# Down projection of a gated FFN: Strassen sums of the weights and of the gated width made by adding transfers, with turned signs

## The chip, the cores and the metric

The kernel runs on one core of one Trainium2 chip. The metric is device time in microseconds (us) of one execution, start to end; lower is better. Engines are named as the profile names them: PE (matrix unit; PEld is its weight loading), DVE (vector), ACT (scalar), POOL (GpSimd) and SP (the queue that issues most transfers). "SPq" is SP issuing a transfer.

## The reference, cut to what matters

One transformer layer on 1024 tokens of width 1024. Only its last part is touched by the change:

```python
def conv_ffn(h, w_up, conv_w, conv_b, w_down):          # h (1, 1024, 1024)
    u = h @ w_up                                        # (1, 1024, 5632)
    acc = conv_b + sum(up[:, j:j + L] * conv_w[j] for j in range(3))   # width-3 depthwise conv over tokens
    a, g = jnp.split(acc, 2, axis=-1)                   # two halves of 2816
    return (jax.nn.silu(g) * a) @ w_down                # the gated width (1, 1024, 2816) @ (2816, 1024)
...
x = x_mid + g2 * conv_ffn(modulate(rms_norm(x_mid, norm2_w), sh2, sc2), w_up, conv_w, conv_b, w_down)
```

All of it is float32. The kernel splits every operand into a high and a low part, so each product of two blocks is three matmuls.

## The kernel before, in words

The stages follow each other: start-up, attention, mLSTM, the two branch projections, the output projection (`project`), and then, in `stage_ffn`, the up projection in 22 **units** and the down projection in 7 **products**.

A unit j (loop `for j in range(NFC)`, NFC = 22) makes 128 channels of `a` and 128 of `g`. `Units.first_mm`, `first_ev` and `rest` run the seven block products of a Strassen scheme on PE into the banks `pa`, `pc`, `pb`; ACT and DVE bring them to the tiles `ua` and `ug` (128 channels x 1024 tokens). `conv_gate(j, ua, ug)` puts the convolution on DVE and ACT (tiles `cv`), multiplies, and stores the gated 128 x 1024 block to the HBM tensor `f_d`. The weights of a unit come in one 1 MB load to a tile `ur`. While the conv of unit j runs on DVE, PE is already in unit j + 1.

The tiles `ua`, `ug`, `cv` and those of the sums come from one pool of eight buffers (`ur`/`accp`, tag "a"), six of them allocated a unit. So what is stored or summed late holds back a tile of about the unit after next.

The down projection multiplies the gated width F (2816 x 1024, in NK = 11 pairs of 128-row blocks k and NK + k, and two token halves `t0`, `t1`) by W (`w_dn`, two column halves). Seven products p = 0..6 read f_d, s1_d, s2_d (HBM: sums of F) and `w_dn` or T (HBM, `wt_d`: four sums of W for each k) in pieces of two k, which `operands` loads and splits. The sums are made during the units:

- `weight_sums(k, ...)`: loads four 128 x 512 blocks of `w_dn`, four DVE subtractions (helper line L1906, 128 x 512 each), four stores to T (L1945). For k = 0, 1, 2 (`E.w_early`) this runs in the output projection, with the loads on ACT's queue; for k = 3..10 in unit k + 1 with all on SP.
- `hidden_sums(k, fb)`, in units 12 to 21 and after the last: loads block k of f_d back (`fa`), four DVE operations on 128 x 512 (L2182 to L2185), two 512 KB stores to s1_d and s2_d.

A framework's scheduler sets the order of each engine's instructions when the program is built, and each engine then takes its instructions in that order. A transfer that has to wait stands at the head of its queue and holds back those behind it.

Of the kernel before, what the change touches and what calls it, by code (L numbers as in the profile page):

```python
# [8 lines left out]
F32 = mybir.dt.float32  # L9
# [4 lines left out]
ALU = mybir.AluOpType  # L14
# [4 lines left out]
P = 128  # L19
D = 1024  # L20
L = 1024
# [14 lines left out]
NFC = DFF // P  # L36
# [1566 lines left out]
def stage_tail(E, st):  # L1603
    nc, tc, A, ident, expo, vecT, dr, out, dbg = E.nc, E.tc, E.A, E.ident, E.expo, E.vecT, E.dr, E.out, E.dbg
# [45 lines left out]
    def x512(name, dt=F32R, pool=None):  # L1650
        if pool is None:
            pool = nx[0] % 56 // 8
            nx[0] += 1
        return xts[pool].tile([P, 512], dt, tag="x", name=name)
# [211 lines left out]
    def square(b, n=1):  # L1866
        if n == 0:
            RS[b] = tp1.tile([P, 4], F32, name=f"rrx{b}")
        rr = RS[b]
        sq = nc.scalar.activation(xj, acc[b][:, n * 512 : (n + 1) * 512], AF.Square, accum_out=rr[:, n : n + 1])  # L1870
        if n == 0:
            return sq
        nc.vector.tensor_scalar(rr[:, 2:3], rr[:, 0:1], rr[:, 1:2], D * EPS, op0=ALU.add, op1=ALU.add)
        nc.gpsimd.tensor_tensor(rr[:, 3:4], rr[:, 2:3], expo[:, 0:1], op=ALU.pow)
# [57 lines left out]

    NK = NFC // 2
    T = dr.tile([P, 4, NK, 512], F32, name="wt_d")
    E.w_early = 3

    def weight_sums(k, a0, a1, b0, b1, eng=None):
        for w, i, o in ((a0, 0, k), (a1, 1, k), (b0, 0, NK + k), (b1, 1, NK + k)):
            (eng or nc.sync).dma_start(w, A["w_dn"][i, :, o])
        sub(a0, a1, a0)  # L1940
        sub(a1, b1, a1)
        sub(b1, b1, a0)
        sub(b0, b0, b1)
        for i, o in enumerate((a0, b1, a1, b0)):
            nc.sync.dma_start(T[:, i, k], o)  # L1945

    psc = E.psx_s
    U = Units(
# [7 lines left out]
    for i, b in enumerate((4, 5, 6, 7, 0, 1, 2, 3)):  # L1956
        project(0, b, w)
        if i == 3:
            held = E.og
        sq = square(b, 0)  # L1960
        if 2 <= i < 2 + E.w_early:
            with tc.issue_after(sq.ins):
                weight_sums(i - 2, *[x512(f"w{x}{i - 2}", F32, 5 + i % 2) for x in range(4)], eng=nc.scalar)
    norm_factors()
    with tc.issue_after(held.ins):
        w = load_w(A["w_o"][1], "wo1", g1b[:, 512:1024], raws=raw)
# [177 lines left out]
def stage_ffn(E, st):  # L2144
# [9 lines left out]

    def conv_gate(j, ua, ug):
        res = []
        for u, ch in ((ua, j), (ug, NFC + j)):
            r = ur.tile([P, L], F32, tag="a", name=f"cv{j}_{ch}")  # L2160

            def cw(i):
                return vecT[:, V_CW + 44 * i + ch : V_CW + 44 * i + ch + 1]

            nc.scalar.activation(r, u, AF.Identity, bias=vecT[:, V_CB + ch : V_CB + ch + 1], scale=cw(1))  # L2165
            nc.vector.scalar_tensor_tensor(r[:, 1:], u[:, : L - 1], cw(0), r[:, 1:], op0=ALU.mult, op1=ALU.add)
            nc.vector.scalar_tensor_tensor(r[:, : L - 1], u[:, 1:], cw(2), r[:, : L - 1], op0=ALU.mult, op1=ALU.add)
            res.append(r)
        a, g = res
        nc.scalar.activation(g, g, AF.Silu)  # L2170
        nc.vector.tensor_tensor(a, a, g, op=ALU.mult)
        nc.sync.dma_start(f_d[j * P : (j + 1) * P], a)
        return a


    t0, t1 = slice(0, 512), slice(512, 1024)
    tt = nc.vector.tensor_tensor

    def hidden_sums(k, fb):
        fa, o = [ur.tile([P, L], F32, tag="a", name=f"f{x}{k}") for x in "as"]  # L2180
        nc.sync.dma_start(fa, f_d[k * P : (k + 1) * P])
        tt(o[:, t0], fa[:, t0], fa[:, t1], op=ALU.subtract)  # L2182
        tt(fa[:, t1], fa[:, t1], fb[:, t1], op=ALU.add)
        tt(fa[:, t0], fa[:, t1], fa[:, t0], op=ALU.subtract)
        tt(o[:, t1], fb[:, t0], fa[:, t0], op=ALU.subtract)  # L2185
        nc.sync.dma_start(s1_d[k * P : (k + 1) * P], fa)
        nc.sync.dma_start(s2_d[k * P : (k + 1) * P], o)

    def rows(src, k0, cs):
        return lambda k, n: src[(k0 + k) * P : (k0 + k + n) * P, cs].rearrange("(k p) t -> p k t", p=P)  # L2190
# [20 lines left out]
    def operands(i):  # L2211

        p, k0, n = pieces[i]
        if i % 7 < 2:
            raw = rawp.tile([P, 2, D], F32, tag="raw", name=f"dr{i}")
            raw = raw[:, 0], raw[:, 1]
        else:
            raw = op4(f"drf{i}", F32), op4(f"drw{i}", F32)
        raw = [r.rearrange("p (k c) -> p k c", k=2) for r in raw]
        out = []  # L2220
        for r, src in zip(raw, PRODS[p]):
            nc.sync.dma_start(r[:, :n], src(k0, n))
        for k in range(n):
            pairs = []
            for r, x in zip(raw, "fw"):
                pr = [E.x512(f"d{x}{y}{i}_{k}", pool=homes[i % len(homes)]) for y in "hl"]
                split_from(nc, *pr, r[:, k])
                pairs.append(pr)
            out.append(pairs)
        return out  # L2230

    def sums(j, a):
        if 0 <= j < NK:
            if j >= E.w_early:
                weight_sums(j, *[w[:, t] for w in [ur.tile([P, L], F32, tag="a", name=f"w{x}{j}") for x in "ab"] for t in (t0, t1)])
        elif j >= NK:
            hidden_sums(j - NK, a)

    a = None
    for j in range(NFC):  # L2240
# [21 lines left out]
    U2 = [E.x512(f"u2_{c}", F32, 3) for c in range(4)]  # L2262
    U4 = [E.x512(f"u4_{c}", F32, 3) for c in range(4)]

    def finish(q, ps, add):

        r, ns = q
        ns = (t0, t1)[ns]
        xm = []
        for c in range(4):  # L2270
            x = dx.tile([P, 512], F32, tag="xm", name=f"xm{q}{c}")
            nc.sync.dma_start(x, xm_d[(4 * r + c) * P : (4 * r + c + 1) * P, ns])
            xm.append(x)
        for c in range(4):
            o = op2(f"o{q}{c}", F32)
            src = ps[c]
            if add is not None:
                tt(o, src, add[c], op=ALU.add)
                src = o
            tt(o, src, g2b[:, ns], op=ALU.mult)  # L2280
            tt(o, o, xm[c], op=ALU.add)
            nc.sync.dma_start(out[(4 * r + c) * P : (4 * r + c + 1) * P, ns], o)
# [32 lines left out]
    for p in range(7):  # L2315

        ps = banks[p] = banks[p - 2] if p in (2, 5, 6) else (yb if p % 2 else xb)(p)
        first = p not in (2, 5, 6)
        ops = []
        if p == 6:  # L2320
            XM = ahead((1, 0), U2)
        while ix < len(pieces) and pieces[ix][0] == p:
            ops += ready[ix] if ix < len(ready) else operands(ix)
            ix += 1
            for _ in range(2 if ix in (5, 8, 11) else 1 if 4 <= ix < 17 else 0):
                last_row()
            if ix == 17:
                for i in (6, 7):
                    mod_row(E, None, i, banks[1][3], U4[2])
                nc.sync.dma_start(g2b, E.g_d[1].to_broadcast([P, D]))  # L2330
            n0 = len(ops) - pieces[ix - 1][2]
            for k in range(n0, min(len(ops), NK - TAIL if p == 6 else NK)):
                (fh, fl), w = ops[k]
                for c in range(4):
                    cs = sl(c * P, P)
                    product(nc, ps[c], [(fh[:, cs], fl[:, cs])], [w], first and k == 0, k == NK - 1)
        if p == 0:
            for c in range(4):
                copy_act(nc, U2[c], ps[c])
        elif p == 1:  # L2340
            for c in range(4):
                tt(U2[c], ps[c], U2[c], op=ALU.add)
        elif p == 2:
            finish((0, 0), ps, None)
        elif p == 3:
            for c in range(4):
                tt(U4[c], ps[c], U2[c], op=ALU.add)
        elif p == 4:
            finish((1, 1), ps, U4)
        elif p == 5:  # L2350
            finish((0, 1), ps, U2)
        else:
            s0, s1 = sl(0, 256), sl(256, 256)
            o, tmp = op2("ol3", F32), op2("olt", F32)
            tt(tmp[:, s1], ps[3][:, s1], g2b[:, s1], op=ALU.mult)
            tt(XM[3][:, s1], XM[3][:, s1], tmp[:, s1], op=ALU.add)
            for c, s, bank in [(c, t0, ps[c]) for c in range(3)] + [(3, s0, ps[3]), (3, s1, banks[5][0])]:
                cs = sl(c * P, P)
                rhs = [(w[0][:, s], w[1][:, s]) for _, w in ops[-TAIL:]]
                product(nc, bank[:, s], [(f[0][:, cs], f[1][:, cs]) for f, _ in ops[-TAIL:]], rhs, s is s1)  # L2360
                r = o if c == 3 else op2(f"ol{c}", F32)
                tt(r[:, s], bank[:, s], g2b[:, s], op=ALU.mult)
                tt(r[:, s], r[:, s], XM[c][:, s], op=ALU.add)
                nc.sync.dma_start(out[(4 + c) * P : (5 + c) * P, s], r[:, s])
    sX.close()

# [82 lines left out]
```

## Time and profile before

| | |
|---|---|
| median of 3 runs | 1844.02 us (1841.78 to 1851.08) |
| the profiled execution | 1849.14 us, its span 1847.4 us |
| granted PE clock, mean over the span | 0.988 |
| PE busy | 1790.8 us, 97% of the span |
| DVE busy | 1425.9 us, 77% |
| ACT busy | 1069.8 us, 58% |
| POOL busy | 508.3 us, 28%; nothing after 1250 us |
| transfers | 342.47 MB, all issued by SP (314.47 MB) and ACT (26.22 MB), none by POOL |

The output projection lies at about 1125 to 1210 us, the units at 1229 to 1650 us, the down projection at 1650 to 1847 us. Times in rows of the trace are us from the span's start unless they are marked ns. In a row of a timeline stand start, length, engine, line and what is written from what; a time behind `[` is idle time of that engine before the row and what ended it.

### The profile page before, as it was taken

How to read it: one execution, taken by the hardware profiler on the slowest of the kernel's cores; microseconds unless marked ns; L12 is line 12 of the kernel's file. 1: busy time of each engine (PE TensorE's matmuls, PEld its weight loads, DVE VectorE, ACT ScalarE, POOL GpSimd, SP SyncE). 2: the span in 40 equal slices, each digit the busy share in tenths (PEclk: the TensorE clock that was granted, in tenths of full speed). 3: DMA queues.
4: the chain of work that ended last, by engine and by line, in shares of the span. 5: the costliest groups of instructions: out<-in, count | busy, mean ns of one | idle time of the engine just before them, and what ended most of it. 6: DMA issues, size and time to landing. Idle time of an engine off the chain costs nothing.

```text
span 1847.4 us, 27864 instructions
## 1 busy us (share of the span) xinstructions
PE 1790.8 (97%) x9207; PEld 1283.5 (69%) x9207; DVE 1425.9 (77%) x2864; ACT 1069.8 (58%) x2229; POOL 508.3 (28%) x747
## 2 busy tenths in 40 slices
PE   7989999999998899999999999999999999999999
PEld 3855555555554566656668887878888888888887
DVE  3858888888788686858687787698889898897665
ACT  4747877878787565645356462476444444465441
POOL 2467769587862530303010020000000000000000
PEclk9999999999999899999999999999999999999999
DMA  9747988888796625261359927322454544599751
GB/s 342 233 138 146 201 170 179 192 180 199 147 182 131 219 79 192 79 213 37 132 188 368 344 92 246 141 77 106 172 207 180 194 160 166 195 318 371 260 172 69
DMA packets 302193, 342.47 MB, mean 185 GB/s; under 512 B 176208, under 2 KB 200672, under 8 KB 299232
## 3 DMA queue, kind: packets, MB, share of 16 engines
q1 hardware_dynamic: 287648, 314.47, 56.3%
q10 hardware_dynamic: 14400, 26.22, 4.2%
q8 instruction: 72, 1.18, 0.3%
q14 instruction: 73, 0.60, 0.1%
HBM read 224.61 MB, written 76.16 MB: 163 GB/s over the span
## 4 chain that ended last, share of the span: by engine, by line
PE 78%; DVE 7%; DMA 4%; issue 3%; ACT 3%; POOL 3%; SPq 0%; ACTq 0%; DVEq 0%; POOLq 0%
PE g L706 8%; PE pq L706 6%; PE pa L2027 4%; PE pa L2029 4%; PE pa L2028 4%; PE po L706 3%; PE dx L2029 2%; PE dx L2027 2%; PE dx L2028 2%; PE pb L2027 2%; PE pb L2029 2%; PE pb L2028 2%; PE yb L2029 2%; PE yb L2027 2%; PE yb L2028 2%
## 5 line engine op out<-in xcount | busy, mean ns | idle before, releaser
L850 DVE CUSTOM_DVE_ANT_0 s<-s,maskA,nsink 128x640 f32<-128x640 f32 (+1 forms) x128 | 117.4, 917 | 65.5 <-PE s L845 65.0
L866 DVE TENSOR_TENSOR P<-s,P 128x640 f16<-128x640 f32 (+1 forms) x128 | 100.6, 786 | 1.0 <-ACT s L861 1.0
L860 ACT ACTIVATE P<-s,st 128x640 f16<-128x640 f32 (+1 forms) x128 | 98.2, 767 | 4.1
L706 PE MATMUL g<-hH,fh 128*128 128x512 f16 x256 | 97.1, 379 | 0.0
L706 PE MATMUL g<-hH,fl 128*128 128x512 f16 x256 | 97.0, 379 | 0.0
L706 PE MATMUL g<-hL,fh 128*128 128x512 f16 x256 | 97.0, 379 | 0.0
L861 ACT ACTIVATE s<-s,st 128x640 f32<-128x640 f32 (+1 forms) x128 | 93.8, 733 | 0.0
L706 PEld LDWEIGHTS <-hH 128*128 128x128 f16 x640 | 62.8, 99 | 37.3 <-issue 1.8
L858 ACT ACTIVATE st<-st,shift 128x1 f32<-128x1 f32 x128 | 37.6, 294 | 85.6 <-DVE st L850 84.8
L706 PE MATMUL pq<-wha,hH 128*128 128x384 f16 (+1 forms) x256 | 84.9, 332 | 0.1
L706 PE MATMUL pq<-wha,hL 128*128 128x384 f16 (+1 forms) x256 | 84.9, 332 | 0.0
L706 PE MATMUL pq<-wla,hH 128*128 128x384 f16 (+1 forms) x256 | 84.9, 332 | 0.0
L706 PEld LDWEIGHTS <-fh 128*128 128x128 f16 x512 | 49.2, 100 | 45.4
L2165 ACT ACTIVATE cv<-ua,vecT 128x1024 f32<-128x1024 f32 x22 | 27.4, 1246 | 84.9 <-DVE ua L2138 84.9
L1436 POOL TENSOR_SCALAR kwh<-k,gcall 128x128 fp32r<-128x128 f32 x72 | 32.5, 455 | 157.2 <-PE dC L164 53.9
L47 ACT ACTIVATE dfh<-drf 128x512 fp32r<-128x512 f32 x55 | 34.4, 628 | 59.3 <-PE dx L2028 26.5
L2027 PE MATMUL dx<-dwh,dfh 128*128 128x512 f32 (+1 forms) x176 | 68.3, 388 | 0.0
L2029 PE MATMUL dx<-dwh,dfl 128*128 128x512 f32 (+1 forms) x176 | 68.2, 388 | 0.0
L2028 PE MATMUL dx<-dwl,dfh 128*128 128x512 f32 (+1 forms) x176 | 68.2, 387 | 0.0
L54 DVE TENSOR_TENSOR dfl<-drf,dfh 128x512 fp32r<-128x512 f32 x55 | 37.6, 688 | 36.1 <-ACT dfh L47 36.1
L165 PE MATMUL kv<-whkv,hL 128*128 128x384 f16 x192 | 62.6, 326 | 0.0
L164 PE MATMUL kv<-wlkv,hH 128*128 128x384 f16 x192 | 62.6, 326 | 0.0
(691 smaller groups left out, 6249.9 us busy)
## 6 DMA issues: line engine op xcount, KB each, us to landing
ur<-in_w_up SPq DMA_DIRECT2D x22, 1024.0 KB
wmb<-in_w_modB SPq DMA_DIRECT2D x48, 256.0 KB
f_d<-cv SPq DMA_DIRECT2D x22, 512.0 KB
wm<-in_w_modA SPq DMA_DIRECT2D x16, 512.0 KB
fr<-in_w_g SPq DMA_DIRECT2D x32, 256.0 KB
drf<-fs_d SPq DMA_DIRECT2D x15, 512.0 KB
drw<-wt_d SPq DMA_DIRECT2D x14, 512.0 KB
w1b<-in_w_cx SPq DMA_DIRECT2D x16, 388.0 KB
```

The lines of the kernel that those rows point to most:

```text
L54: rest = nc.vector.tensor_tensor(lo, src, whole, op=ALU.subtract)
L164: nc.tensor.matmul(ps, lh[:, ls], rl[:, rs], start=False, stop=False)
L165: nc.tensor.matmul(ps, ll[:, ls], rh[:, rs], start=False, stop=stop and i == n - 1)
L706: nc.tensor.matmul(self.ps, x, w, start=self.i == 0, stop=self.i == self.n - 1)
L850: nc.vector.tensor_tensor_reduce(e, e, self.mask, scale=self.ss[:, h : h + 1], scalar=nsink[:, hh : hh + 1], op0=ALU.add, op1=ALU.min, acc ...
L858: nc.scalar.activation(m, st4[:, 8 + h : 9 + h], AF.Identity, bias=shift)
L860: nc.scalar.activation(two[:, :W], e, AF.Exp, bias=m, scale=-1.0)
L861: nc.scalar.activation(e, e, AF.Exp, bias=m, scale=-1.0, accum_out=st4[:, 4 + h : 5 + h])
L866: nc.vector.tensor_tensor(two[:, W : 2 * W], self.e[h], two[:, :W], op=ALU.subtract)
L2027: nc.tensor.matmul(ps, lh, rh, start=start and i == 0, stop=False, skip_group_check=True)
L2028: nc.tensor.matmul(ps, lh, rl, start=False, stop=False, skip_group_check=True)
L2029: nc.tensor.matmul(ps, ll, rh, start=False, stop=stop and i == n - 1, skip_group_check=True)
```

## The change

Weight sums: two blocks are loaded to the two halves x, y of one tile `ws`; the others are added to them by transfers that POOL issues with an add at the destination (`accum_op=ALU.add`), and after each stage the half is stored to T. All eleven k run in the units. Sums of the gated width: of a block j, DVE makes one difference u = a[t1] - a[t0]; blocks j < 11 are stored to s1_d and s2_d as they come, and those of j >= 11 are added to what stands there by POOL's transfers. The loading back of f_d is gone, and the t1 half of blocks j < 11 isn't stored to f_d.

For subtractions to become additions, the conv's weights and bias of channels 11 x 128 and up of the value half are negated once (four POOL operations on `vecT`), so those gated blocks have the other sign; signs are turned back in the split of product 2 (`scale=-1.0`) and in the last operations (`subtract` for `add`).

```diff
-    E.w_early = 3
-
-    def weight_sums(k, a0, a1, b0, b1, eng=None):
-        for w, i, o in ((a0, 0, k), (a1, 1, k), (b0, 0, NK + k), (b1, 1, NK + k)):
-            (eng or nc.sync).dma_start(w, A["w_dn"][i, :, o])
-        sub(a0, a1, a0)
-        sub(a1, b1, a1)
-        sub(b1, b1, a0)
-        sub(b0, b0, b1)
-        for i, o in enumerate((a0, b1, a1, b0)):
-            nc.sync.dma_start(T[:, i, k], o)
+    for o, n in ((V_CB, 1), (V_CW, 3)):
+        for i in range(n):
+            v = vecT[:, o + 44 * i + NK : o + 44 * i + NFC]
+            nc.gpsimd.tensor_scalar(v, v, -1.0, None, op0=ALU.mult)
+
+    def weight_sums(k, x, y):
+        src = lambda n, o: A["w_dn"][n, :, o + k]
+        add = lambda o, i: nc.gpsimd.dma_start(o, i, accum_op=ALU.add)
+        nc.sync.dma_start(x, src(0, 0))
+        nc.sync.dma_start(y, src(1, NK))
+        add(x, src(1, 0))
+        add(y, src(1, 0))
+        nc.sync.dma_start(T[:, 0, k], x)
+        nc.sync.dma_start(T[:, 2, k], y)
+        add(x, src(1, NK))
+        nc.sync.dma_start(T[:, 1, k], x)
+        add(x, src(0, NK))
+        nc.sync.dma_start(T[:, 3, k], x)
...
-        nc.sync.dma_start(f_d[j * P : (j + 1) * P], a)
+        if j < NK:
+            nc.sync.dma_start(f_d[j * P : (j + 1) * P, t0], a[:, t0])
+        else:
+            nc.sync.dma_start(f_d[j * P : (j + 1) * P], a)
...
-    def hidden_sums(k, fb):
-        fa, o = [ur.tile([P, L], F32, tag="a", name=f"f{x}{k}") for x in "as"]
-        nc.sync.dma_start(fa, f_d[k * P : (k + 1) * P])
-        tt(o[:, t0], fa[:, t0], fa[:, t1], op=ALU.subtract)
-        tt(fa[:, t1], fa[:, t1], fb[:, t1], op=ALU.add)
-        tt(fa[:, t0], fa[:, t1], fa[:, t0], op=ALU.subtract)
-        tt(o[:, t1], fb[:, t0], fa[:, t0], op=ALU.subtract)
-        nc.sync.dma_start(s1_d[k * P : (k + 1) * P], fa)
-        nc.sync.dma_start(s2_d[k * P : (k + 1) * P], o)
+    def hidden_sums(j, a):
+        k = j % NK
+        u = ur.tile([P, L], F32, tag="a", name=f"fu{j}")[:, t0]
+        tt(u, a[:, t1], a[:, t0], op=ALU.subtract)
+        r = slice(k * P, (k + 1) * P)
+        twice = lambda x: x[:, None, :].to_broadcast([P, 2, 512])
+        halves = lambda x: x[r].rearrange("p (s t) -> p s t", s=2)
+        if j < NK:
+            nc.sync.dma_start(s1_d[r, t1], a[:, t1])
+            nc.sync.dma_start(s1_d[r, t0], u)
+            nc.sync.dma_start(halves(s2_d), twice(u))
+        else:
+            nc.gpsimd.dma_start(halves(s1_d), twice(a[:, t1]), accum_op=ALU.add)
+            nc.gpsimd.dma_start(s2_d[r, t1], u, accum_op=ALU.add)
...
     def sums(j, a):
         if 0 <= j < NK:
-            if j >= E.w_early:
-                weight_sums(j, *[w[:, t] for w in [ur.tile([P, L], F32, tag="a", name=f"w{x}{j}") for x in "ab"] for t in (t0, t1)])
-        elif j >= NK:
-            hidden_sums(j - NK, a)
+            w = ur.tile([P, L], F32, tag="a", name=f"ws{j}")
+            weight_sums(j, w[:, t0], w[:, t1])
+        if j >= 0:
+            hidden_sums(j, a)
```

**SP's queue around the end of unit 7's conv, before.** `f_d` is the store of a gated block, `ur11` the weights of unit 11, `wa7`/`wb7` the four blocks of `w_dn` for k = 7, `wt_d` is T. In brackets stand the semaphores that a row waits for: DMAHW of transfers issued by SP or ACT, the rest of engines.

```order
L2172 DMA f_d_14761<-cv7_7_15789 128x1024 [waits DMAHW4_49,DVE_49]
L2055 DMA ur11_16186<-in_w_up 128x2048 [waits DMAHW5_49,DVE_49,Activation_49]
L1939 DMA wa7_15920<-in_w_dn 128x512 [waits DMAHW6_49]
L1939 DMA wa7_15920<-in_w_dn 128x512 [waits DMAHW7_49]
L1939 DMA wb7_15921<-in_w_dn 128x512 [waits DMAHW1_49,DMAHW0_49]
L1939 DMA wb7_15921<-in_w_dn 128x512
L1945 DMA wt_d_13770<-wa7_15920 128x512 [waits DMAHW2_49,DVE_49]
L1945 DMA wt_d_13770<-wa7_15920 128x512 [waits DMAHW3_49,DVE_49]
L1945 DMA wt_d_13770<-wb7_15921 128x512 [waits DMAHW4_49,DVE_49]
L1945 DMA wt_d_13770<-wb7_15921 128x512 [waits DMAHW5_49,DVE_49]
L2172 DMA f_d_14761<-cv8_8_15934 128x1024 [waits DMAHW6_49,DVE_49]
```

**The same place of SP's queue with the change.** DMASW are semaphores of POOL's adding transfers; `ws7` is the tile of k = 7, `fu7` the difference u of block 7, `fs1`/`fs2` are s1_d and s2_d.

```order
L2180 DMA f_d_14717<-cv7_7_15801 128x512 [waits DMAHW2_49,DVE_49]
L2194 DMA fs1_d_14718<-cv7_7_15801 128x512 [waits DMAHW3_49]
L2059 DMA ur11_16202<-in_w_up 128x2048 [waits DMAHW4_49,DVE_49,Activation_49]
L1952 DMA wt_d_13770<-ws6_15785 128x512 [waits DMAHW5_49,DMASW3_49]
L1943 DMA ws7_15932<-in_w_dn 128x512 [waits DMAHW6_49]
L1944 DMA ws7_15932<-in_w_dn 128x512 [waits DMAHW7_49]
L2195 DMA fs1_d_14718<-fu7_15943 128x512 [waits DMAHW0_49,DVE_49]
L2196 DMA fs2_d_14719<-fu7_15943 256x1x512 [waits DMAHW1_49]
L1947 DMA wt_d_13770<-ws7_15932 128x512 [waits DMAHW2_49,DMASW4_49]
L1948 DMA wt_d_13770<-ws7_15932 128x512 [waits DMAHW3_49,DMASW5_49]
L1950 DMA wt_d_13770<-ws7_15932 128x512 [waits DMAHW4_49,DMASW6_49]
L2180 DMA f_d_14717<-cv8_8_15948 128x512 [waits DMAHW5_49,DVE_49]
```

The four T stores that waited for DVE now wait for POOL's transfers, and the last one of k = 6 (L1952) stands ahead of the loads of k = 7: from k = 3 on, each k's chain of transfers has to end before the next k's begins.

**POOL's queue in the same stretch, with the change** (before, the small operation L1874 on `rrx7`, ahead of the units, is POOL's last row). L1942 is the adding transfer into a `ws` tile.

```order
L1942 DMA ws6_15785<-in_w_dn 128x512 [waits DMAHW1_49,DMASW3_49,DMASW2_49]
L1942 DMA ws7_15932<-in_w_dn 128x512 [waits DMAHW5_49,DMAHW6_49,DVE_49,Activation_49]
L1942 DMA ws7_15932<-in_w_dn 128x512 [waits DMAHW7_49,DMASW5_49]
L1942 DMA ws7_15932<-in_w_dn 128x512 [waits DMAHW2_49,DMASW4_49]
L1942 DMA ws7_15932<-in_w_dn 128x512 [waits DMAHW4_49,DMASW7_49,DMASW6_49]
L1942 DMA ws8_16079<-in_w_dn 128x512 [waits DMAHW0_49,DMAHW1_49,DVE_49,Activation_49]
```

Of the three adds into one half, the second and third each wait for the store of the one before (DMAHW2 and DMAHW4 are the T stores L1947 and L1950 above). For blocks 11 and up POOL's rows are in turn L2198 (512 KB added to s1_d) and L2199 (256 KB added to s2_d).

**ACT's queue at unit 9's first copies, before.** `ua9` and `ug9` are what unit 9 brings out of the banks `pa9` and `pb9`, `cv8_30` the second half of unit 8's conv.

```order
L2165 ACTIVATE cv8_30_15938<-ug8_15830,vecT_68 128x1024 [waits DMAHW6_49,DMAHW3_49,DMAHW7_49,DMAHW2_49,Activation_49]
L47 ACTIVATE ua9_15971<-pa9_15945 128x512 [waits PE_49]
L2170 ACTIVATE cv8_30_15938<-cv8_30_15938 128x1024 [waits DVE_49,Activation_49]
L47 ACTIVATE ua9_15971<-pa9_15945 128x512 [waits PE_49]
L47 ACTIVATE q2h10_16057<-s34_10_16054 128x1024 [waits DVE_49]
L47 ACTIVATE ug9_15975<-pb9_15974 128x512 [waits DMAHW4_49,PE_49]
```

**The same rows with the change.**

```order
L2172 ACTIVATE cv8_30_15952<-ug8_15842,vecT_68 128x1024 [waits Activation_49]
L47 ACTIVATE ua9_15985<-pa9_15959 128x512 [waits DMAHW3_49,DMAHW2_49,PE_49]
L2177 ACTIVATE cv8_30_15952<-cv8_30_15952 128x1024 [waits DVE_49,Activation_49]
L47 ACTIVATE ua9_15985<-pa9_15959 128x512 [waits PE_49]
L47 ACTIVATE q2h10_16071<-s34_10_16068 128x1024 [waits DVE_49]
L47 ACTIVATE ug9_15989<-pb9_15988 128x512 [waits DMAHW0_49,DMASW3_49,DMAHW5_49,DMASW1_49,PE_49]
```

Before, `ug9` waits for the store of gated block 7 (DMAHW4, as in SP's rows above); now already `ua9`, an earlier row, waits for the two stores of that block (DMAHW2 and DMAHW3), and `ug9` for the last store and adds of k = 6.

More of the change, by code (lines that the diff above doesn't have):

```diff
@@ L1959, in stage_tail @@
             held = E.og
[L1960 to L1963, printed above, removed]
+        square(b, 0)
     norm_factors()
@@ L2153, in stage_ffn @@
     rawp, op4, op2 = E.rawp, E.op4, E.op2
+    t0, t1 = slice(0, 512), slice(512, 1024)
+    tt = nc.vector.tensor_tensor
     def conv_gate(j, ua, ug):
@@ L2171, in conv_gate @@
         nc.vector.tensor_tensor(a, a, g, op=ALU.mult)
-        nc.sync.dma_start(f_d[j * P : (j + 1) * P], a)
-        return a
-    t0, t1 = slice(0, 512), slice(512, 1024)
-    tt = nc.vector.tensor_tensor
-    def hidden_sums(k, fb):
-        fa, o = [ur.tile([P, L], F32, tag="a", name=f"f{x}{k}") for x in "as"]
-        nc.sync.dma_start(fa, f_d[k * P : (k + 1) * P])
-        tt(o[:, t0], fa[:, t0], fa[:, t1], op=ALU.subtract)
-        tt(fa[:, t1], fa[:, t1], fb[:, t1], op=ALU.add)
-        tt(fa[:, t0], fa[:, t1], fa[:, t0], op=ALU.subtract)
-        tt(o[:, t1], fb[:, t0], fa[:, t0], op=ALU.subtract)
-        nc.sync.dma_start(s1_d[k * P : (k + 1) * P], fa)
-        nc.sync.dma_start(s2_d[k * P : (k + 1) * P], o)
+        if j < NK:
+            nc.sync.dma_start(f_d[j * P : (j + 1) * P, t0], a[:, t0])
+        else:
+            nc.sync.dma_start(f_d[j * P : (j + 1) * P], a)
+        return a
+    def hidden_sums(j, a):
[12 more added lines that the diff above has]
+            nc.gpsimd.dma_start(s2_d[r, t1], u, accum_op=ALU.add)
     def rows(src, k0, cs):
@@ L2226, in operands @@
                 pr = [E.x512(f"d{x}{y}{i}_{k}", pool=homes[i % len(homes)]) for y in "hl"]
-                split_from(nc, *pr, r[:, k])
+                split_from(nc, *pr, r[:, k], scale=-1.0 if p == 2 and x == "f" else None)
                 pairs.append(pr)
@@ L2263, in stage_ffn, with finish @@
     U4 = [E.x512(f"u4_{c}", F32, 3) for c in range(4)]
-    def finish(q, ps, add):
+    def finish(q, ps, add, op=ALU.add):
         r, ns = q
@@ L2277, in finish @@
             if add is not None:
-                tt(o, src, add[c], op=ALU.add)
+                tt(o, src, add[c], op=op)
                 src = o
@@ L2346, in stage_ffn @@
             for c in range(4):
-                tt(U4[c], ps[c], U2[c], op=ALU.add)
+                tt(U4[c], ps[c], U2[c], op=ALU.subtract)
         elif p == 4:
@@ L2350, in stage_ffn @@
         elif p == 5:
-            finish((0, 1), ps, U2)
+            finish((0, 1), ps, U2, ALU.subtract)
         else:
@@ L2355, in stage_ffn @@
             tt(tmp[:, s1], ps[3][:, s1], g2b[:, s1], op=ALU.mult)
-            tt(XM[3][:, s1], XM[3][:, s1], tmp[:, s1], op=ALU.add)
+            tt(XM[3][:, s1], XM[3][:, s1], tmp[:, s1], op=ALU.subtract)
             for c, s, bank in [(c, t0, ps[c]) for c in range(3)] + [(3, s0, ps[3]), (3, s1, banks[5][0])]:
@@ L2362, in stage_ffn @@
                 tt(r[:, s], bank[:, s], g2b[:, s], op=ALU.mult)
-                tt(r[:, s], r[:, s], XM[c][:, s], op=ALU.add)
+                tt(r[:, s], XM[c][:, s], r[:, s], op=ALU.subtract)
                 nc.sync.dma_start(out[(4 + c) * P : (5 + c) * P, s], r[:, s])
```

## The prediction

> **What bounds the kernel now.** I read the page's first lines, then busy time by stage, then what PE waits for, then SP's queue in one unit.
>
> ```profile
> span 1847.4 us, 27864 instructions
> PE 1790.8 (97%) x9207; PEld 1283.5 (69%) x9207; DVE 1425.9 (77%) x2864; ACT 1069.8 (58%) x2229; POOL 508.3 (28%) x747
> ```
>
> PE is busy for 97% of the span, DVE for 77%. Those are averages, so the busy time of each engine in the stages that the change touches (columns: stretch, length, PE, PEld, DVE, ACT, POOL with counts, granted clock, share of the transfer engines, GB/s):
>
> ```profile
> 1000.00:1050.00 50.00, 50.00 (x223) 41.40 (x222) 40.07 (x66) 27.77 (x54) 0.00 (x0) 1.00 1.02 378
> ...
> 1125.00:1200.00 75.00, 74.87 (x345) 61.47 (x344) 47.93 (x75) 26.45 (x52) 3.32 (x6) 1.00 0.56 206
> 1200.00:1229.00 29.00, 27.38 (x135) 22.04 (x134) 26.11 (x69) 22.33 (x55) 3.02 (x2) 1.00 0.16 55
> 1287.00:1440.00 153.00, 153.00 (x677) 126.69 (x676) 135.80 (x160) 73.88 (x90) 0.00 (x0) 1.00 0.51 190
> 1440.00:1650.00 210.00, 210.00 (x928) 173.90 (x927) 188.62 (x234) 107.11 (x140) 0.00 (x0) 1.00 0.54 199
> 1650.00:1715.00 65.00, 65.00 (x292) 53.90 (x291) 46.04 (x75) 31.99 (x57) 0.00 (x0) 1.00 0.94 344
> 1715.00:1841.60 126.60, 126.60 (x566) 104.91 (x565) 76.39 (x124) 40.53 (x70) 0.00 (x0) 1.00 0.48 164
> 1841.60:1847.40 5.80, 2.18 (x19) 1.98 (x17) 2.93 (x6) 0.00 (x0) 0.00 (x0) 0.90 0.37 137
> ```
>
> In the units (1287 to 1650) and the down projection PE is busy every microsecond. That a busy PE is not PE at its peak is no objection: it starts 677 matmuls in 153.0 us, 4.4 a us, with DVE 89% busy, and 566 in 126.6 us, 4.5 a us, with DVE 60% busy. PE's pace doesn't follow DVE's load. Around the change PE stands still only here:
>
> ```profile
> PE op L164 <- DVE wo0l L54: 0.6, 1, 0.6
> ...
> PE x2p L1913 <- DVE acc L1877: 1.4, 1, 1.4
> ```
>
> The first waits for the split of an output weight, the second for a tile that a store releases (4.77 us in the chain, below). The change touches neither.
>
> **The change, part by part.** Five terms, in the profiled execution's own time of 1849.14 us, 5.1 above the median of 1844.02.
>
> *DVE's sums.* Four subtractions for each k, and four operations for each hidden pair, go; one difference u for each of 22 blocks comes.
>
> ```profile
> L1906 DVE TENSOR_TENSOR w<-w,w x12: 681/688/693, 1138.4 to 1156.7; 128x512 f32<-128x512 f32 x12
> L1906 DVE TENSOR_TENSOR wa<-wa x8: 681/683/693, 1307.5 to 1440.8; 128x512 f32<-128x512 f32 x8
> ...
> L2182 DVE TENSOR_TENSOR fs<-fa x11: 680/683/692, 1459.8 to 1639.7; 128x512 f32<-128x512 f32 x11
> ```
>
> 12 + 32 + 44 = 88 operations of 0.684 us go, 22 come: 45.1 us less of DVE, 2.05 us a unit. On the path that is 0: PE has no idle time there to give back. ACT's twelve loads of early blocks stand in a stretch with 74.87 of 75.00 us of PE; at most 0.13 us.
>
> *Signs.* The four negations on POOL wait only for `vecT`, and POOL is idle then; product 2's split becomes a scaled one in a stretch where DVE works 60%. Both 0.
>
> ```profile
> L367 DVE COPY vecT<-pv x1: 424/424/424, 4.2 to 4.2; 128x256 f32<-128x256 f32 x1
> ...
> 12.40 0.19 POOL L393 TENSOR_SCALAR ss<-ss 128x1 f32<-128x1 f32 x1 [11.43 <-ACT xj L392]
> ```
>
> They end before 12.40 if each takes no more than 1.9 us ((12.40 - 4.6) / 4); POOL's row here takes 0.19.
>
> *Traffic.* A unit before moved 3.67 MB:
>
> ```profile
> DMA packets 1440, 3.67 MB, mean 193 GB/s; under 512 B 160, under 2 KB 160, under 8 KB 1312
> ```
>
> In units of 1 MB that was `ur` 1, four blocks loaded 1, T 1, f_d 0.5: 3.5. With the change it is `ur` 1, two blocks 0.5, four adds 1, T 1, f_d 0.25, s1_d 0.5, s2_d 0.5: 4.75, or 5.75 if an add counts its destination again. The share of 0.51 goes to 0.69 to 0.84. At a share of 1.02 (1000:1050) PE is still busy 50.00 of 50.00. Cost 0.
>
> *The chain of one k.* This is the term that can cost. SP's queue and ACT's in one unit before:
>
> ```profile
> 1394.03 0.32 SPq L2172 DMA_DIRECT2D f_d<-cv  x1
> 1395.87 0.33 SPq L2055 DMA_DIRECT2D ur<-in_w_up  x1
> 1396.26 0.90 SPq L1939 DMA_DIRECT2D wa<-in_w_dn  x2
> ...
> 1403.41 2.33 SPq L1945 DMA_DIRECT2D wt_d<-wa  x2
> ...
> 1413.07 0.32 SPq L2172 DMA_DIRECT2D f_d<-cv  x1
> ...
> 1406.56 0.60 ACT L47 ACTIVATE ua<-pa 128x512 f32<-128x512 f32 x1
> ```
>
> A unit lasts 1413.07 - 1394.03 = 19.04 us. With the change each k is a row of transfers that wait for each other: load, add, store T0, add, store T1, add, and only then T3 and the next k's loads, all in SP's order, with the next block's f_d store behind T1. For k = 3..10 the cycle is load + 3 A + 2 stores + one issue of 0.33, where A is one add of 256 KB from POOL's waiting row to its landing. Prices of waited-for transfers from the chain:
>
> ```profile
> 803.61 2.00 DMA t_at_d<-t_at
> ...
> 818.14 2.85 DMA s_bm<-in_w_bm
> ...
> 1210.17 4.77 DMA xm_d<-acc
> ```
>
> A 256 KB store takes 2.00 and a 256 KB load 2.85, so the cycle is 2.85 + 3 A + 4.00 + 0.33 = 7.18 + 3 A, and it fits into 19.04 us while A is at most 3.95. No transfer in this trace is issued by POOL or adds. Its lower bound is the load of the same bytes, 2.85. Its upper bound, for an add that reads its destination too, is the 512 KB store, 4.77. I take 2.85, plus another 0.26 MB at 378 GB/s, 0.69, plus one small POOL operation of 0.19 to 0.55: an estimate of 3.7 to 4.1, nearer the load, since only bytes and an issue are added to it. That is at the edge of fitting: the cycle is 18.3 to 19.5.
>
> The Trainium skill (DMA: Bandwidth & Descriptors, Anatomy of one DMA) gives a GpSimd-issued transfer about 2.0 us + bytes / 436e3; with 0.52 MB read that would be an estimated 3.2 us and a cycle of 16.8. No run here shows it; the sum doesn't use it.
>
> What is late when the chain is too long? f_d's store, behind T1, holds the buffer that ACT's first copy of the unit after next takes (1406.56 in the rows); PE then waits for its bank. Stored at 1394.03, landed 2.00 to 4.77 later, a second issue of 0.33 behind: the cushion is 7.4 to 10.2 us, I take 8.5. The cycle overruns by 3 A - 11.86 a unit, eight times. Loss = 8 (3 A - 11.86) - 8.5, never under 0: nothing up to A = 4.31, 9 us at 4.69, 11 us at 4.77. The `ur` loads have three units in hand and only follow. At 3.7 to 4.1 the loss is 0.
>
> *Blocks 11 to 21.* Two adds a unit into HBM. Twice the 512 KB row, 9.5 us, is within the unit, SP no longer waits for DVE there, and product 1 reads s1_d only after product 0, whose 132 matmuls (11 blocks x 4 x 3) last 132 / 4.5 = 29 us. Cost 0.
>
> Sum: 1849.14 + 0, against the median 1844.02 + 0; I say 1845, for a wait of a microsecond at the first units.
>
> **Rivals.** *The chain is longer than a unit (slower).* Place: T1 and T3 in SP's queue from k = 3; it decides above A = 4.69. For it: three adds in a row, each behind its own store, and the upper bound is past that point. Against: 4.77 is twice the bytes with a queue ahead of it. At A = 5.2 the loss is 8 x 3.74 - 8.5 = 21, the time 1866.
>
> *POOL is held up by DVE (slower).* POOL's eight equal small operations, and DVE's row beside the slow one:
>
> ```profile
> L1874 POOL TENSOR_TENSOR rrx<-rrx,expo x8: 548/550/2469, 1169.0 to 1211.7; 128x1 f32<-128x1 f32 x8
> ...
> 1212.20 1.22 DVE L54 TENSOR_TENSOR r1l<-ur,r1h 128x1024 fp32r<-128x1024 f32 x1
> ```
>
> One took 2.47 us, 1.92 more, while DVE worked without a gap on two-input operations like those of the units. If every add of POOL pays that, A = 3.9 + 1.92 = 5.8, the loss 8 x 5.6 - 8.5 = 36, the time 1880. Against: the one slow operation reads its tile, and seven of eight weren't slow. The Trainium skill (SBUF — State Buffer, the trap that DVE blocks DMA) warns that GpSimd can't write its descriptors while DVE holds the shared port, and adds that two-input DVE operations hold up only GpSimd reads. By the first half this rival wins, by the second it falls; the slow row agrees with the second, and no run here has shown a POOL-issued transfer.
>
> *DVE was the bound after all (faster).* The 45.1 us would come back: 1799. Against it stand the two paces above; only a PE idle time of 0.13 + 1.62 us (first rows) is in reach.
>
> **How the numbers follow.** About 0.5%, 9 us, is what a measurement of this kernel tells from no change. A up to 4.69, the chain hidden: 0.68, 1845. Chain too long by itself: 0.20. POOL held up: 0.08. DVE the bound: 0.04. The range runs from 1839 (PE's 1.7 us given back, and the lowest run before, 1841.78, less that and a little) to 1880, the second rival's time; beyond it lies about 0.08 above and 0.04 below. The likeliest case by itself is 1840 to 1853.
>
> **What would show it.** In the changed kernel: DVE's busy share of 1287:1650 near 0.78; PE busy all of each stretch up to the end; SP's waits on T stores (L1947 to L1952) of 2 to 4 us each; `f_d<-cv` rows 19.0 us apart. Wrong would be: PE or ACT waiting in the units for a transfer out of a gated block, f_d rows over 20 us apart for k = 3..10 and 19 again after, or POOL's add rows of several us.

## The result, and the profile after

The changed kernel takes 1903.6 us (median; 1903.1 to 1909.37) against 1846.24 (1841.78 to 1851.08) for the kernel before beside it: 1.032 times as long, 95% interval 1.028 to 1.035, or 57 us. 1845 was predicted. The profiled execution took 1909.37 us, its span 60.2 us more than before.

From the page of the changed kernel, its first lines, the queue of POOL's transfers (packets, MB, share of 16 engines' span) and the chain that ended last:

```profile
span 1907.6 us, 27893 instructions
PE 1810.7 (95%) x9207; PEld 1294.6 (68%) x9207; DVE 1389.5 (73%) x2798; ACT 1068.9 (56%) x2229; POOL 569.8 (30%) x817
...
q0 software_dynamic: 10912, 20.19, 6.9%
...
PE 71%; DMA 11%; DVE 7%; issue 4%; POOL 3%; ACT 3%; SPq 0%; ACTq 0%; POOLq 0%; DVEq 0%
```

PE is busy 19.9 us longer for the same 9207 matmuls, so it stands still about 40 us more. Transfers are now 11% of the chain, against 4% before. Busy time by stage (columns as before: stretch, length, PE, PEld, DVE, ACT, POOL, granted clock, share of the transfer engines, GB/s):

```profile
1287.00:1440.00 153.00, 131.67 (x540) 106.01 (x538) 101.94 (x113) 60.03 (x73) 21.27 (x24) 0.93 0.74 199
1440.00:1525.00 85.00, 70.90 (x288) 56.87 (x288) 51.44 (x57) 30.22 (x37) 13.54 (x15) 0.92 0.78 206
...
1715.00:1841.60 126.60, 126.60 (x568) 105.02 (x568) 79.54 (x129) 57.20 (x103) 0.00 (x0) 1.00 0.80 280
```

Where the kernel before starts 677 matmuls in 1287 to 1440, this one starts 540. From 1715 to 1841.6, in the down projection, PE is busy throughout. What was waited for (total us, times, longest):

```profile
POOL ws L1942 <- DMA wt_d<-ws: 140.5, 22, 8.9
...
ACT ua L47 <- DMA fs_d<-cv: 42.4, 8, 7.4
...
PE pa L2031 <- ACT ua L47: 29.1, 9, 5.7
```

Read from the bottom: PE waits for ACT's first copy `ua` (29.1 us; most of the rest are waits for the copies to `ug`, 12.6), that copy waits for the store of a gated block (the second one, to s1_d, which stands directly behind f_d's), and POOL's adds wait for the T stores. SP's queue and POOL's in one unit show why the gated block is late:

```profile
1397.23 0.42 SPq L1943 DMA_DIRECT2D ws<-in_w_dn  x1
...
1405.47 0.33 SPq L1947 DMA_DIRECT2D wt_d<-ws  x1
...
1413.18 0.32 SPq L1950 DMA_DIRECT2D wt_d<-ws  x1
1413.59 0.38 SPq L2180 DMA_DIRECT2D f_d<-cv  x1
...
1414.56 0.40 SPq L2059 DMA_DIRECT2D ur<-in_w_up  x1
1422.26 0.32 SPq L1952 DMA_DIRECT2D wt_d<-ws  x1
1422.63 0.42 SPq L1943 DMA_DIRECT2D ws<-in_w_dn  x1
```

```profile
1401.18 1.77 POOL L1942 DMA_DIRECT2D ws<-in_w_dn  x2 [9.75 <-DVE q2l L54]
1408.98 0.89 POOL L1942 DMA_DIRECT2D ws<-in_w_dn  x1 [6.03 <-DMA wt_d<-ws]
1415.86 0.89 POOL L1942 DMA_DIRECT2D ws<-in_w_dn  x1 [5.99 <-DMA wt_d<-ws]
```

From one load of `ws` (L1943) to the next, 1397.23 to 1422.63, are 25.40 us: load to first add 3.95, add to T0 4.29, T0 to second add 3.51, add to T1 4.20, T1 to third add 2.68, add to T3 6.40, T3 to next load 0.37. These links close on themselves; a unit of PE work takes 19.04. The trace puts the end of POOL's wait at 1401.18 down to DVE; in the units before and behind it is the load, after 4.92 and 3.66 us, so I count the link as the load's. f_d's store leaves 0.41 us after T1, once in 25 us. Two links from the chain that ended last (start, length, what; "issue" is time for which the trace shows no wait):

```profile
1405.47 2.87 DMA wt_d<-ws
1408.38 0.60 issue
1408.98 4.18 DMA ws<-in_w_dn
```

The store lands after 2.87 us, and 0.60 more go by until POOL's row begins.

The first and the thirteenth f_d row (blocks 0 and 12), of the kernel before and then of the changed one:

```profile
1253.07 0.33 SPq L2172 DMA_DIRECT2D f_d<-cv  x1
...
1470.72 0.32 SPq L2172 DMA_DIRECT2D f_d<-cv  x1
```

```profile
1251.91 0.33 SPq L2180 DMA_DIRECT2D f_d<-cv  x1
...
1523.08 0.39 SPq L2182 DMA_DIRECT2D f_d<-cv  x1
```

That is 217.65 us before and 271.17 after: 53.5 of the 60.2 us between the two profiled executions lie between these two rows, while weights are summed. Behind them the gaps are 19.0 us again, after one of 25.4, which holds most of the remainder. I use this stretch, called "blocks 0 to 12" below, as a second measure of the experiments.

### The profile page after: what moved, and what is told of

The parts are those of the page before. It is cut to its first block, busy times and chain, and to the rows that moved or that the text cites. A ratio compares the mean times of both kernels' runs of the same rounds, so it can differ in the third digit from the quotient of the medians.

```text
span 1907.6 us, 27893 instructions
## 1 busy us (share of the span) xinstructions
PE 1810.7 (95%) x9207; PEld 1294.6 (68%) x9207; DVE 1389.5 (73%) x2798; ACT 1068.9 (56%) x2229; POOL 569.8 (30%) x817
## 4 chain that ended last, share of the span: by engine, by line
PE 71%; DMA 11%; DVE 7%; issue 4%; POOL 3%; ACT 3%; SPq 0%; ACTq 0%; POOLq 0%; DVEq 0%
PE g L706 7%; PE pq L706 6%; DMA ws<-in_w_dn 4%; PE po L706 3%; PE pa L2031 3%; PE pa L2032 3%; PE pa L2033 3%; PE dx L2031 2%; PE dx L2033 2%; PE dx L2032 2%; PE yb L2031 2%; PE yb L2032 2%; PE yb L2033 2%; PE kv L163 2%; PE kv L164 2%
## 5 line engine op out<-in xcount | busy, mean ns | idle before, releaser
L1942 POOL DMA_DIRECT2D ws<-in_w_dn x44 | 39.2, 926 | 264.1 <-DMA wt_d<-ws 140.5
L47 ACT ACTIVATE ua<-pa 128x512 f32<-128x512 f32 x44 | 26.3, 597 | 88.9 <-PE pa L2033 44.9
L2031 PE MATMUL pa<-t2h,q1h 128*128 128x512 f32 x84 | 38.1, 453 | 29.1 <-ACT ua L47 29.1
```

Of the source, the lines that this page charges most:

```text
L47: return nc.scalar.activation(out, in_, AF.Copy, scale=scale)
L1942: add = lambda o, i: nc.gpsimd.dma_start(o, i, accum_op=ALU.add)
L2031: nc.tensor.matmul(ps, lh, rh, start=start and i == 0, stop=False, skip_group_check=True)
```

## The experiments

Theory A: the loss is a wait in a queue. Each k is a serial chain of adds and stores, longer than a unit; SP takes its rows in order, so the gated blocks and sums behind the chain leave late and hold the buffers of the next units. Theory B: adding transfers cost time wherever they are, by their bytes or their load on the transfer engines. Theory C: POOL and DVE hold each other up.

### One half of the change at a time

The first kernel makes the weight sums with DVE (all eleven k in the units, with additions), and keeps the adding transfers for the gated width:

```diff
-            w = ur.tile([P, L], F32, tag="a", name=f"ws{j}")
-            weight_sums(j, w[:, t0], w[:, t1])
+            weight_sums_dve(j, *[w[:, t] for w in [ur.tile([P, L], F32, tag="a", name=f"w{x}{j}") for x in "ab"] for t in (t0, t1)])
```

> Weight sums on DVE again (four loads, four additions, four stores to T on SP), but in the units for all eleven k; the sums of the gated width stay adding transfers. Theory A (SP waits in order for each k's serial chain of adds and stores, 25.4 us a k against a unit of 19 us, and so the gated blocks leave late): the f_d stores come 19 to 20 us apart again and the time is 1845, between 1841 and 1850. Theory B (the adding transfers as such, by their bytes or by load on the transfer engines, slow the units): the hidden sums' 33 adds keep a part, 1855 to 1880. Theory C (POOL and DVE hold each other up): also a part, 1855 to 1880.

Measured: 1846.91, 1.0009 times the kernel before (0.9997 to 1.002). Blocks 0 to 12 take 219.04 us. The 22 adding transfers into HBM (33 in the expectation, which counts them in 256 KB) and DVE's relief from the hidden sums together change the time by no more than 0.2%.

The second keeps the weight chains and makes the hidden sums as before (a load of f_d, four DVE operations, two stores).

> Weight sums by adding transfers exactly as changed; the sums of the gated width go back to a load of f_d, four DVE operations and two stores. Theory A: the chain of the weights stands as it is, so the whole loss stays, 1895 to 1910, with f_d stores 25 us apart. Theories B and C: fewer adding transfers, less loss, 1865 to 1890.

Measured: 1912.25 (1.0346 to 1.0385), 2 us above A's range and 9 above the changed kernel; blocks 0 to 12 take 284.49, 13 more than there. The loss goes with the weight chains. The excess is the same kind of wait: the first load of f_d (`fa`) stands right behind the last chain's T3 in SP's queue, and DVE, in order, waits for it once for 25.9 us; PE then stands still for 22.1.

### Every other chain

```diff
+            if j % 2:
+                weight_sums_dve(j, *[w[:, t] for w in [ur.tile([P, L], F32, tag="a", name=f"w{x}{j}") for x in "ab"] for t in (t0, t1)])
+            else:
+                w = ur.tile([P, L], F32, tag="a", name=f"ws{j}")
+                weight_sums(j, w[:, t0], w[:, t1])
```

> Weight sums by adding transfers for the even k only (six chains), on DVE for the odd k. Theory A: a chain of 25.4 us overruns its unit by 6.4 us, under the cushion of 7 to 10 us, and the next unit, without a chain, gives it back: 1845 to 1855. Theories B and C (a cost for each adding transfer): six elevenths of the loss stay, 1872 to 1882.

Measured: 1881.07 (1.0169 to 1.0213), a miss for A's number and inside the range of B and C: six of eleven chains kept 35 of 57 us. Blocks 0 to 12 take 253.88. The chain that ended last, around an odd k of this kernel (start, length, what):

```profile
1354.70 4.26 DMA ws<-in_w_dn
1358.99 0.32 SPq L1952
...
1360.82 6.96 DMA wa<-in_w_dn
1367.87 0.69 DVE wa L1955
...
1379.40 0.32 SPq L2191
```

The odd k's loads stand behind the even k's last store (L1952). DVE, which also takes its rows in order, then waits for them ahead of the conv, so the next f_d (L2191) leaves 27.0 us after the one before. The overrun isn't given back in the next unit: it is handed on to a second queue. This run alone doesn't tell A from B.

### The same transfers in another queue

Loads, adds and T stores of the weights all go to POOL's queue and into `g2b`, a tile that is idle in the units, so SP waits for none of them. A two-column copy of gated block k on DVE and one on POOL hold each k in its unit. In `weight_sums` every `nc.sync` becomes `nc.gpsimd`, and:

```diff
+            E.tok[j] = E.tp1.tile([P, 2], F32, name=f"tok{j}")
+            nc.vector.tensor_copy(E.tok[j], a[:, 0:2])
...
-            w = ur.tile([P, L], F32, tag="a", name=f"ws{j}")
-            weight_sums(j, w[:, t0], w[:, t1])
+            nc.gpsimd.tensor_copy(g2b.rearrange("p (s t) -> p s t", s=2)[:, :, 0:1], E.tok.pop(j)[:, :, None])
+            weight_sums(j, g2b[:, t0], g2b[:, t1])
```

> The same transfers for the weight sums, loads, adds and stores to T, but all in POOL's queue and in a tile that nothing else uses during the units (each k still starts after gated block k, by a two-column copy on DVE and one on POOL); SP waits for none of them. Theory A: the gated blocks leave on time whatever the chain takes, 1843 to 1852, with f_d stores 19 us apart. Theories B and C: the adds are all there, so the loss stays, 1880 to 1910.

Measured: 1964.99 (1.0632 to 1.067), far above both. Two waits and two stretches of this kernel tell why:

```profile
DVE fu L2191 <- DMA fs_d<-cv: 116.7, 1, 116.7
...
PE pa L2031 <- DVE ug L2140: 114.8, 1, 114.8
```

```profile
1287.00:1440.00 153.00, 153.00 (x676) 126.69 (x675) 125.20 (x148) 75.38 (x91) 34.28 (x49) 1.00 0.69 205
1475.00:1588.00 113.00, 0.00 (x0) 0.00 (x0) 1.25 (x2) 0.00 (x0) 32.61 (x49) 0.51 0.47 105
```

While the chains run, PE is busy 153.00 of 153.00 us; blocks 0 to 12 take 216.73. Then everything stops once, for 115 us: the first adds of the gated width (block 11) stand in POOL's queue behind chains that start 31.9 us apart on average and have fallen that far behind. I had thought of SP's queue and not of the one the transfers went to. The next kernel takes only that away: the hidden sums are made with DVE, as before the change.

> All transfers of the weight sums (loads, 44 adds, stores to T) in POOL's queue as in the run before, one chain after the other (31.2 us a k there, ending near 1600 us), and the sums of the gated width made by a load and four DVE operations again, so that nothing of the units stands behind POOL's chains. Theory A (a loss only where gated blocks or their sums wait in a queue behind a chain): PE never waits, 1843 to 1850, though each chain is 12 us longer than a unit. Theory B (44 adding transfers into SBUF cost time as such): 1880 or more.

Measured: 1851.43, 1.0026 (1.0015 to 1.0037).

```profile
1287.00:1440.00 153.00, 153.00 (x677) 126.69 (x676) 120.09 (x140) 74.62 (x90) 35.01 (x53) 1.00 0.61 170
1440.00:1600.00 160.00, 159.64 (x701) 130.97 (x700) 137.88 (x165) 75.26 (x93) 42.19 (x50) 1.00 0.72 227
```

All 44 adds into SBUF are made in the units, in chains longer than before (they start 29 to 40 us apart), and PE works through. Together with the first experiment, which has the other 22 adds, this refutes B and C for 52 of the 57 us; the 4.8 that stay (2.8 to 6.8 by the interval) I didn't trace. The cost of a chain depends on what stands behind it.

This kernel takes the chains out of SP's queue and out of the pool of eight buffers at once, so a rival is that the tile `ws`, held for the length of a chain, was the loss. The trace of the changed kernel gives it a small part: ACT's copies waited 9.5 us for T stores that hold `ws`, and the copies to `ua` 42.4 for a gated block's store. And in the last experiment, with chains in `g2b` but in SP's queue, six chains still cost 30 us.

### What a link costs

The 44 adds become plain copies of the same bytes (the additions of the weights are left out), by POOL and then by SP:

```diff
-        add = lambda o, i: nc.gpsimd.dma_start(o, i, accum_op=ALU.add)
+        add = lambda o, i: nc.gpsimd.dma_start(o, i)
```

> The changed kernel with the 44 adds of the weight sums replaced by plain copies of the same 256 KB by POOL into the same places (the additions of the weights are left out). It prices the add itself. In the run with all on POOL a waited-for load took 2.96 us from the end of its issue and an add 4.25: so each link gets 1.3 us shorter, the cycle 25.4 - 3 x 1.3 = 21.5 us, and by theory A the time 1850 to 1875. If reading the destination costs nothing, the cycle and 1903 stay.

> The same plain copies (the additions of the weights are left out), issued by SP instead of POOL: prices POOL's issue (0.88 us a row against 0.33, and its start). Theory A: another 0.5 us a link, the cycle near 20 us, 1845 to 1865, at or below the run with POOL's copies.

Measured, one execution each: 1866.81 and 1842.1; blocks 0 to 12 take 237.09 and 216.71. The first is where A put it, the second 3 us below its range. Median time from issue to landing by the page, of the changed kernel's adds and then of POOL's copies (queue, count, KB, us):

```profile
ws<-in_w_dn POOLq DMA_DIRECT2D x44, 256.0 KB, 5.2
```

```profile
ws<-in_w_dn POOLq DMA_DIRECT2D x44, 256.0 KB, 3.4
```

And the middle of a chain with SP's copies:

```profile
1401.51 0.33 SPq L1947 DMA_DIRECT2D wt_d<-ws  x1
...
1403.54 0.33 SPq L1942 DMA_DIRECT2D ws<-in_w_dn  x1
1406.18 0.32 SPq L1950 DMA_DIRECT2D wt_d<-ws  x1
```

Here the store takes 2.03 us (1401.51 to 1403.54) and the copy 2.64. With adds by POOL the same two links took 3.51 and 4.20. So in one unit the add for a copy, its issue by POOL, and the way between POOL and SP make some 1.5 us a link. From one load of `ws` (L1943) to the next, the chain here takes 19.33 and 18.30 us, about a unit; with POOL's copies it takes 21.3 to 22.5, with the adds, from 1371 us on, 24.6 to 26.1. The change from add to copy and the change from POOL to SP are each worth some 3 us a chain.

### Two attempts to shorten the chain

Four tiles for each k, so that no add waits for a store, then four stores:

```diff
+        for w, s in ((a0, src(0, 0)), (a1, src(1, NK)), (b1, src(1, NK)), (b0, src(0, NK))):
+            nc.sync.dma_start(w, s)
+        add(a0, src(1, 0))
+        add(a1, src(1, 0))
+        add(b1, a0)
+        add(b0, b1)
+        for i, o in ((0, a0), (2, a1), (1, b1), (3, b0)):
+            nc.sync.dma_start(T[:, i, k], o)
```

> Four tiles for each k instead of two, so that no add waits for a store: four loads on SP, two adds from w_dn side by side, then two adds from tile to tile (W00+W10 onto W11, that onto W01), then four stores. Again 44 adds into SBUF, and SP still waits for them in order. Cycle by theory A: load 3.95 + 3 adds in a row x 4.3 + 0.33 = 17.2 us, inside the unit of 19: 1843 to 1855, f_d stores 19 us apart. Theory B (a cost for each add): 1890 to 1910.

Measured: 1887.0 (1.0207 to 1.0238), a miss for A's number, a little under the range of B: f_d rows are mostly 22 to 24 us apart and not 19, and blocks 0 to 12 take 254.74. It is better than the change by 17 us, as the shorter chain asks, but one link grew:

```profile
1386.16 0.39 SPq L2057 DMA_DIRECT2D ur<-in_w_up  x1
1386.65 1.07 SPq L1944 DMA_DIRECT2D wa<-in_w_dn  x2
```

```profile
1393.43 1.79 POOL L1942 DMA_DIRECT2D wa<-in_w_dn  x2 [11.07 <-DMA wa<-in_w_dn]
```

From load to first add it is 6.78 us, right behind the 1 MB `ur`; the third add of the change (6.40) also stands right behind it. So `ur` was moved to ACT's queue, in the changed kernel and in this one:

```diff
-        self.nc.sync.dma_start(raw, self.src(j))
+        (self.nc.scalar if j > 3 else self.nc.sync).dma_start(raw, self.src(j))
```

> The changed kernel with the 1 MB loads ur from unit 4 on issued by ACT instead of SP, so that they no longer start right after f_d's store and beside the third add. Theory: the third add (6.40 us beside ur, against 4.29 and 4.20) falls to about 4.3, the cycle from 25.2 to about 23, and the time to 1870 to 1890. If the third add is long for another reason: no change, 1895 to 1910.

> The kernel with four tiles for each k and no store between the adds (1887, f_d stores 23.1 us apart), with the ur loads from unit 4 on issued by ACT. There the loads of w_dn stood right behind ur in SP's queue and took 6.8 us before the first add. Theory: they fall to 3 to 4 us, the cycle to 19 to 20 us, and the time to 1848 to 1865. If ur is not the reason: 1880 to 1890.

Measured: 1918.92 (1.0353 to 1.0444) and 1879.37 (1.0155 to 1.0214). Both miss: the first goes the other way, the second ends just under the 1880 to 1890 that were to mean that `ur` isn't the reason. In the first, ACT issues `ur` at 1389.65 and 1410.89, and the adds around them are:

```profile
1390.21 0.90 POOL L1942 DMA_DIRECT2D ws<-in_w_dn  x1 [8.41 <-DMA wt_d<-ws]
1399.11 0.88 POOL L1942 DMA_DIRECT2D ws<-in_w_dn  x1 [8.00 <-DMA wt_d<-ws]
1409.30 1.77 POOL L1942 DMA_DIRECT2D ws<-in_w_dn  x2 [9.31 <-DMA ws<-in_w_dn]
```

```profile
1396.45 0.32 SPq L1950 DMA_DIRECT2D wt_d<-ws  x1
1403.27 0.32 SPq L1952 DMA_DIRECT2D wt_d<-ws  x1
...
1419.29 0.32 SPq L1948 DMA_DIRECT2D wt_d<-ws  x1
```

The third add is short now, 4.16 us (1399.11 to 1403.27, T3's row), as expected; but the second, beside `ur`, takes 6.24, and the add into `y`, the second of the two from 1409.30 on, more than 8 (its T2 store waits until 1419.29). In these units the slow link moves with the 1 MB load. Besides, f_d's row now stands behind T3 (L1952) and not behind T1, so the whole chain delays it. In the second, the load took 3.96 us where `ur` lay well ahead, and 6.51 where it lay near; the adds of these two units took 3.6 to 6.1, a spread that I can't ascribe to one transfer.

### Every other chain again, with the odd loads ahead

The loads for an odd k are issued a unit earlier, ahead of the even k's chain, and that chain uses `g2b` and the two-column copies.

> Adding transfers for the even k and DVE for the odd k, as in the run that gave 1881, but the four loads of an odd k are issued a unit earlier, before the chain of the even k (whose tile is now one that nothing else uses, started by a two-column copy on DVE and one on POOL). Theory: there DVE stood 8 us in order waiting for loads that SP could issue only after the chain; with the loads there in time the overrun of a chain is given back in the next unit: 1845 to 1860. If each adding transfer has its own cost: 1875 to 1885.

Measured: 1873.53 (1.0126 to 1.0171), again above A's range and just under the other's; blocks 0 to 12 take 239.91. DVE's longest wait for those loads fell from 8.4 to 5.3 us, and 8 us of the 35 went. But f_d rows now come 12.0 to 14.5 and 26.7 to 30.3 us apart in turn: the first of a pair leaves behind T3 of a chain that takes 27 us, 10 us too late, which is all of the cushion or more. That a late unit spoils the pair fits A; that these pairs cost 30 us and not 0 says that the buffers bear less overrun than I assumed.

## Why the prediction was wrong

Its mechanism was there as the first rival (0.20 at 1866), but not its size. The forecast failed at one term: the chain of one k, sized at 18.3 to 19.5 us and so at a loss of 0, is 25.40, and the loss 57 us.

- **The prices in the chain.** Load 2.85, stores 2.00 each and A = 3.9 gave 18.9 us. Measured in one unit: load 3.95 (1.1 more), two stores 6.19 (2.2 more), three adds 14.89, that is A = 4.96 (3.2 more). So A, on which I set the whole uncertainty, is half of the error; the prices that I held fixed are the other half. They came from transfers at 804 and 818 us. Here a waited-for store has 0.60 us more behind it until POOL's row begins (the chain above); what the transfers beside them add isn't shown apart. For an add by itself 3.9 was too low: in the stop of 115 us, where only POOL's transfers ran, an add landed after 4.2 us (median of two), and chains started 25.6 and 25.9 us apart. My upper bound for A, 4.77, was the lone 512 KB store; an add beside `ur` took 6.40.
- **The loss from the chain.** With 25.40 in place of 7.18 + 3 A, the same formula gives 8 x (25.40 - 19.04) - 8.5 = 42 us; with A = 4.96 alone it gives 16. It counted k = 3 to 10; but the first three chains were also too long: the first three f_d gaps are 20.0, 19.7, 19.9 us against 13.2, 14.9, 17.5 before, another 14. Together 56, near the 57; the closeness is in part luck, since the cushion of 8.5 was a choice and the gaps from k = 3 on are 23.4 to 27.1 and not all 25.4.
- **Who waits.** Right in the main: ACT's first copy `ua` for the gated block's store, then PE (29.1 of about 42 us).
- **The Trainium skill's estimate.** DMA: Bandwidth & Descriptors, Anatomy of one DMA, gave an estimated 3.2 us an add; this trace disagrees, with 4.20 to 6.40 in the unit above and a median of 5.2. For a plain copy of 256 KB the same formula gives an estimated 2.6, against the median of 3.4 above.
- **DVE's relief worth 0.** Nothing speaks against it: the first experiment has 22 of the 66 operations less and gains nothing. DVE's busy time fell by 36.4 us, not 45.1; where the rest went I didn't follow.
- **Signs, blocks 11 to 21, more bytes: 0.** Right: 126.60 of 126.60 us in the down projection, 19.0 us gaps without chains, and PE working through with the 44 adds made in POOL's queue. In the chain, though, an add lasts longer than a copy of the same 256 KB.
- **POOL held up by DVE.** Not seen: POOL's 44 add rows took 0.863 to 1.227 us, median 0.882, beside the same two-input DVE operations. POOL's two-column copies, which read a tile, were held up: in the second run with POOL's queue they took 0.186 to 3.664 us, the longest while DVE made two-input operations. So the slow row that the rival rested on was no sign for transfers.

No version that makes all the sums beat the kernel before: PE works through there already.

## What to carry to other kernels

When DVE work is replaced by adding transfers, size the longest serial chain in an in-order queue against the period of what stands behind it, with prices from transfers that run beside others and cross queues, and give a bound that lies past the worst row, not at it. A chain too long costs little in a queue and a tile of its own (4.8 us here), if nothing in the period stands behind it there; so ask that of the new queue as well. Halving the number of chains or moving one load doesn't cure it when each remaining chain still overruns the buffers' slack.

## What the runs showed of the hardware

PE's pace falls after a wait. A row of PE in the changed kernel (behind the bracket its wait), and the chain that ended last from there on:

```profile
1417.99 0.79 PE L2031 MATMUL pa<-t2h,q1h 128*128 128x512 f32 x1 [4.57 <-ACT ua L47]
```

```profile
1413.18 0.32 SPq L1950
...
1417.34 0.61 ACT ua L47
...
1419.21 0.43 PE pa L2033
...
1423.05 0.43 PE pa L2033
1423.48 0.31 PE pb L2031
1423.79 0.23 PE pb L2032
```

Behind the first, matmuls come 0.43 us apart up to 1423.48, then 0.23; the granted clock is 0.92 to 0.93 over the stretch. This makes most of the 19.9 us of additional busy time: at the pace before, 153.00 us for 677, the 540 matmuls of the first stretch above would take 9.6 us less, and the 288 of the second 5.8. In the run with the one stop of 115 us the granted clock was 0.51 over it. The Trainium skill (TensorE: Matmul & The Clock Gate, Part 1) states that the array idles at half clock and returns to full after a busy window of about 3.4 us; the trace agrees on the half pace, but it lasts 5.5 us here (1417.99 to 1423.48). I take it that it cost little by itself, since the chain of 25.4 us set the unit; no run shows it apart.

An add keeps the transfer engines longer than a copy: between 1290 and 1500 us POOL's queue moved 8.48 MB in 26.2% of the engines' time in the changed kernel, 11.00 MB in 18.4% with plain copies (four adds of the gated width among them): 154 and 285 GB/s while its packets ran.
